# One level of Strassen's algorithm for the gate and up products of 20 of 22 column chunks per FFN, and an order planned with other matmul prices

## The chip, the cores and the metric

The kernel runs on one core of a Trainium2 chip. The metric is the device time of one execution in microseconds (us); before the change its median is 1421.67 us. TensorE multiplies matrices, VectorE, ScalarE and GpSimd work on tiles elementwise, and SyncE (SP in the profile) issues the DMA transfers between the chip's memory (DRAM) and SBUF. TensorE reads its operands from SBUF and writes its sums into PSUM, of which this kernel uses 8 banks of 128 x 512 numbers.

## The reference

A trunk of two layers on 512 tokens of width 1024, in float32. Each layer has a mixer (attention of one kind or another), a cross attention to 256 memory tokens, and an FFN; each adds its normed output to x. Only the FFN and the norm ahead of it are touched:

```python
def swiglu(h, wg, wu, wd):
    return (jax.nn.silu(h @ wg) * (h @ wu)) @ wd

for layer in range(DEPTH):
    ...
    y = swiglu(rms_norm(x, g[4]), ffn_wg[layer], ffn_wu[layer], ffn_wd[layer])
    x = x + rms_norm(y, g[5])
```

wg and wu are 1024 x 2816, wd is 2816 x 1024. The width 2816 is cut into 22 chunks of 128 columns.

## The kernel before

**Two numbers for one.** TensorE takes fp32r operands. To keep float32's precision, every operand is split into a high part (ScalarE's copy into fp32r) and a low part (VectorE's subtraction); `split` (line 556) issues the two. `mm` (line 509) then makes three matmuls of one: high by high, high by low, low by high, each with a weight load of its own. All partitions are 128, and the sum over 1024 has 8 steps (`KO`).

**The FFN** (`ffn`, line 999). `hT` holds the normed activations, transposed: 8 steps x 512 tokens, high and low. `up(c)` makes chunk c: it loads 128 columns of wg and of wu (`w_group`: one raw buffer of 512 KB each, of three; split into high and low, two w buffers each, of eight), and multiplies each with hT into a PSUM bank of its own, 8 steps x 3 matmuls with 512 moving columns. Chunks 0 and 1 go in two halves of 256 tokens, as the first half of hT is ready earlier. Then come tanh on ScalarE, two VectorE steps that read PSUM, and a split whose subtraction is GpSimd's. Three chunks make a group (four in the last). After the next group's first chunk come the group's down products: for each block of 128 tokens and each half of the 1024 output columns a bank, into which the group's chunks are summed, 3 matmuls each of 512 columns, and which VectorE adds to `yacc` (ScalarE copies it in the first group).

**The way to the FFN.** Four blocks of 128 tokens go through `chain` (line 849): out projection, cross attention, norm. Its last stage, `norm_T` (line 632), scales a block, transposes it into two banks (`turn`) and splits each into hT.

**Buffers.** Tiles are taken by tag: raw 3 x 1024 numbers a partition, w 8 x 1024, u 20 x 1024 (activations of chunks, yacc, gains, some down weights), q 10 x 512, pt 4 x 1024 (down weights), and 8 PSUM banks.

**The order.** Nothing is issued while the program is written. `Plan.note` (line 135) records each instruction with what it depends on and a price in ns from `price` (line 182). `order` then simulates the engines, the buffers and the DMA queue in rounds: a backward pass gives each instruction a latest time, a forward pass starts on each engine what is ready, by that time; the best round's order is issued. `lend` (line 398) gives a VectorE addition, subtraction or product on SBUF to GpSimd, when GpSimd has nothing to do and the wait on VectorE is long. The order of each engine is fixed with that; on the chip only semaphores decide when an instruction starts. All instructions are issued by line 491, so the profile's rows tell them apart by tiles: `w` weights, `raw` loaded weights, `ps` PSUM, `q` and `u` the tags above.

Of the kernel before, what the change touches and what calls it, by code (L numbers as in the profile page):

```python
# [11 lines left out]
F32 = mybir.dt.float32  # L12
# [7 lines left out]
P = 128  # L20
# [67 lines left out]
class Plan:  # L88
# [46 lines left out]
    def note(self, eng, method, args, kw):  # L135
        aps = [("out" if i == 0 else "in", v) for i, v in enumerate(args) if isinstance(v, bass.AP)]
        if "out" in kw or "out_" in kw:
            aps = [("in", v) for _, v in aps]
        aps += [("out" if k in ("out", "accum_out") else "in", v) for k, v in kw.items() if isinstance(v, bass.AP)]

        op = dict(eng=eng.name, call=(eng, method, args, kw), cost=0.0, deps=set(), tiles=set(), prio=len(self.ops))
        i = len(self.ops)
        for kind, ap in aps:
            if ap.space == bass.MemoryType.DRAM and not str(ap.tensor.name).startswith("xsave"):
                continue
            name, p0, p1, mask = self.region(ap)
# [35 lines left out]
    def price(self, eng, method, args, kw, aps):  # L182
        n = max([self.free(a) for a in aps] + [1])
        if method == "dma_start":
            size = 1
            for _, k in aps[0].ap:
                size *= k
            return size * 4 / 360.0
        if eng == "tensor":
            if method == "transpose":  # L190
                return 107.0
            c = self.free(args[2]) / 2.4
            return max(25.0, 2.5 + (c if args[2].dtype == F32R else 4 * c))
        if eng == "scalar":
            extra = sum(isinstance(kw.get(k), bass.AP) for k in ("bias", "scale", "accum_out"))
            return (52 if aps[1].space == PSUM else 95) + 0.83 * n + 93 * extra
        if eng == "vector":
            psum = any(a.space == bass.MemoryType.PSUM for a in aps)
            n = n + 62 * sum(isinstance(v, bass.AP) and self.free(v) == 1 for v in args[2:3])
            if method == "reciprocal":  # L200
                return 60 + 8 * n
            if method in ("tensor_copy", "tensor_scalar", "memset") and not psum:
                return 65 + 0.52 * n
            return 65 + 1.04 * n
# [289 lines left out]
class Trunk:  # L494
# [11 lines left out]
    def tile(self, shape, dtype, tag, bufs=1):  # L506
        return self.nc.tile(self.sb, shape, dtype, tag, bufs)

    def mm(self, ps, L, R, first, last):
        (lh, ll), (rh, rl) = L, R  # L510
        mmul = self.nc.tensor.matmul
        mmul(ps, lh, rh, start=first, stop=False)
        mmul(ps, lh, rl, start=False, stop=False)
        mmul(ps, ll, rh, start=False, stop=last)

    def unit(self, dtype=F32R):
        return self.tile([P, 1024], dtype, "u", 20)
# [114 lines left out]
    def norm_T(self, src, g, dst, tb):  # L632

        r = self.rstd(src)
        hs = [self.qtile() for _ in range(2)]
        for i in range(2):
            self.nc.vector.scalar_tensor_tensor(hs[i], src[i], r, g[:, i * 512:(i + 1) * 512], op0=ALU.mult, op1=ALU.mult)
        self.turn(hs, dst, tb)

    def hT_tiles(self):  # L640
        return [self.tile([P, KO, T], F32R, f"hT{k}") for k in ("hi", "lo")]
# [207 lines left out]
    def chain(self, tb, c):  # L849
# [84 lines left out]
        yield  # L934
        if c["hT"] is None:
            c["hT"] = self.hT_tiles()
        self.norm_T(self.xhalves(x, tb), c["g"][2], c["hT"], tb)
        yield

    def first_heads(self, w, c):  # L940
# [24 lines left out]
    def last_heads(self, l, w, units, n, c, x_src, fill):  # L965


        a = self.a
        lead = LEAD if n > 2 else 1
        step = 8.0 / n  # L970

        def before():
            yield from fill
            yield from self.first_heads(w, c)
            c["g"] = [self.gain(a["sandwich_g"][l, 1:2, :])]
            c["wq"] = self.w_group(a["ca_wq"][l], 0, MEM, self.gcols(l))

        def block(tb):
            if tb == 0:
                c["x"] = []  # L980
            x = self.xtile()
            self.nc.sync.dma_start(x, x_src[tb * P:(tb + 1) * P, :])
            c["x"].append(x)
            yield from self.chain(tb, c)

        def rest():
            c["wo"] = [self.w_cols(a["ca_wo"][l], 0, 1, 1024, k) for k in range(2)]
            c["g"] += [self.gain(a["sandwich_g"][l, i:i + 1, :]) for i in (3, 4)]
# [7 lines left out]
        return c["x"], c["hT"]  # L996


    def ffn(self, l, x, hT):
        nc, a = self.nc, self.a  # L1000
        groups = [list(range(c, min(c + 3, NCH))) for c in range(0, NCH - 1, 3)]
        groups[-1].append(NCH - 1)
        acts = {}

        def up(c):
# [4 lines left out]
            for s in parts:  # L1010
                for ps, wf in ((pg, wg), (pu, wu)):
                    for ko in range(KO):
                        self.mm(ps[:, s], wf(ko), (hT[0][:, ko, s], hT[1][:, ko, s]), ko == 0, ko == KO - 1)
            th, b = self.qtile(), self.qtile()
            nc.scalar.activation(th, pg, AF.Tanh, scale=0.5)
            nc.vector.scalar_tensor_tensor(th, th, 1.0, pg, op0=ALU.add, op1=ALU.mult)
# [2 lines left out]
            nc.scalar.activation(at[:, 0:512], b, AF.Copy)  # L1019
            nc.gpsimd.tensor_sub(at[:, 512:1024], b, at[:, 0:512].bitcast(F32))  # L1020

        where = self.pt_tiles
        yacc = None
        up(0)
        for gi, grp in enumerate(groups):
            last = gi == len(groups) - 1
            for c in grp[1:]:
                up(c)
# [4 lines left out]
            if last:  # L1033
                g = self.gain(a["sandwich_g"][l, 5:6, :])
            else:
                up(groups[gi + 1][0])
# [557 lines left out]
    def run(self):  # L1594
# [4 lines left out]
        x, hT = self.mixer0(x)  # L1599
        blocks = self.ffn(0, x, hT)  # L1600
        x, hT = self.mixer1(x, blocks)
        for tb in self.ffn(1, x, hT):
# [43 lines left out]
```

## Time and profile before

| | |
|---|---|
| median of 3 runs | 1421.67 us (1420.76 to 1422.24) |
| the profiled execution | 1422.67 us |
| its span, first to last instruction | 1421.0 us |
| granted TensorE clock, mean | 0.996 |
| TensorE matmul busy | 1383.2 us (97%) |
| VectorE, ScalarE, GpSimd busy | 833.7, 725.0, 355.9 us |
| DMA moved | 132.05 MB, mean 93 GB/s |

The profile is one execution. Its times are us from the first instruction. PE is TensorE, PEld its weight loads, DVE VectorE, ACT ScalarE, POOL GpSimd. A matmul's row lasts longer than the time to the next matmul's start, since matmuls are pipelined: 0.39 us against 0.23 us for 512 columns. So throughput is read from starts and not from durations. A group `x2` of the timeline gives the start of the first and the time to the end of the last.

### The profile page before, as it was taken

Reading aid. Unit: us, or ns where it says so; the run is one execution under the profiler, and the core shown is the slowest. Engines: PE = TensorE matmul, PEld = TensorE weight load, DVE = VectorE, ACT = ScalarE, POOL = GpSimd, SP = SyncE. Lnnn points to the kernel's source line nnn. Section 1 sums busy time; section 2 is a strip of 40 time slices with the busy share of each in tenths; the row PEclk is TensorE's granted clock in tenths of the full one; section 3 lists DMA queues with packets and bytes.
Section 4 is the critical chain, followed back from the end, with each engine's and each line's share of the span. In section 5 each row is a group of like instructions: output and inputs, shape, how many; then the busy total and the mean of one; then the engine's idle time right before and its main releaser. Section 6 shows DMA issues by size and latency. Waiting matters only on the chain.

```text
span 1421.0 us, 21566 instructions
## 1 busy us (share of the span) xinstructions
PE 1383.2 (97%) x8003; PEld 1204.0 (85%) x8003; DVE 833.7 (59%) x1851; ACT 725.0 (51%) x1606; POOL 355.9 (25%) x429
## 2 busy tenths in 40 slices
PE   7999999999899999999999999999989999999997
PEld 6788988889788888888889999988878888888886
DVE  5667899498842333433466888876984233343344
ACT  5768879488643122223245677786863322222322
POOL 2203334244320121012031233312552012101202
PEclk9999999999999999999999999999999999999999
DMA  7251112321233233324321321243234323332411
GB/s 218 65 150 47 46 45 87 107 74 61 89 119 89 89 104 90 114 78 134 105 74 54 95 91 61 77 147 104 85 92 121 89 84 110 89 108 85 119 60 60
DMA packets 150425, 132.05 MB, mean 93 GB/s; under 512 B 6928, under 2 KB 134096, under 8 KB 150320
## 3 DMA queue, kind: packets, MB, share of 16 engines
q1 hardware_dynamic: 150320, 130.67, 30.2%
q8 instruction: 63, 1.03, 0.3%
q14 instruction: 42, 0.34, 0.1%
HBM read 126.26 MB, written 4.19 MB: 92 GB/s over the span
## 4 chain that ended last, share of the span: by engine, by line
PE 84%; DVE 7%; ACT 3%; DMA 2%; POOL 2%; issue 2%; SPq 0%; POOLq 0%; DVEq 0%; ACTq 0%
PE ps L491 84%; DVE q L491 2%; DVE x L491 1%; DVE u L491 1%; ACT q L491 1%; DVE c L491 1%; DMA raw<-in_ev_w_in_dram 1%; POOL c L491 1%; POOL q L491 1%; ACT u L491 1%; DVE pt L491 1%; DMA pt<-in_ev_w_in_dram 0%; DVE w L491 0%; ACT pt L491 0%; POOL x L491 0%
## 5 line engine op out<-in xcount | busy, mean ns | idle before, releaser
L491 PE MATMUL ps<-hThi,w 128*128 128x512 f32 (+1 forms) x1664 | 488.0, 375 | 2.6 <-DVE q L491 2.6
L491 PEld LDWEIGHTS ps<-hThi,w 128*128 128x128 f32 x1664 | 306.5, 190 | 58.3 <-ACT junk L491 1.6
L491 PE MATMUL ps<-hTlo,w 128*128 128x512 f32 (+1 forms) x832 | 311.6, 375 | 0.4 <-DVE hTlo L491 0.2
L491 PE MATMUL ps<-w,hThi 128*128 128x256 f32 (+2 forms) x1280 | 281.9, 316 | 2.3 <-ACT hThi L491 2.3
L491 DVE TENSOR_TENSOR w<-raw,w 128x1024 fp32r<-128x1024 f32 (+1 forms) x136 | 170.2, 1268 | 152.3 <-issue 72.8
L491 ACT ACTIVATE w<-raw 128x1024 fp32r<-128x1024 f32 (+1 forms) x153 | 158.4, 1051 | 164.4 <-PE ps L491 138.7
L491 PE MATMUL ps<-pt,u 128*128 128x512 f32 (+3 forms) x1126 | 231.8, 338 | 1.4 <-DVE pt L491 0.8
L491 PEld LDWEIGHTS ps<-w,hThi 128*128 128x128 f32 x1280 | 210.5, 192 | 15.2 <-ACT hThi L491 3.2
L491 DVE TENSOR_TENSOR u<-ps,u 128x512 f32<-128x512 f32 (+6 forms) x278 | 150.6, 546 | 116.4 <-PE ps L491 98.0
L491 PEld LDWEIGHTS ps<-pt,u 128*128 128x128 f32 (+1 forms) x1126 | 175.2, 173 | 31.6 <-DVE pt L491 1.5
L491 POOL TENSOR_TENSOR u<-q,u 128x512 fp32r<-128x512 f32 x44 | 64.0, 1454 | 542.7 <-ACT u L491 542.7
L491 PE MATMUL ps<-w,hTlo 128*128 128x256 f32 (+2 forms) x640 | 199.8, 313 | 0.0
L491 PE MATMUL ps<-u 128*128 128x512 f32 (+4 forms) x806 | 186.4, 348 | 0.1
L491 PEld LDWEIGHTS ps<-hTlo,w 128*128 128x128 f32 x832 | 158.0, 190 | 28.3 <-DVE hTlo L491 1.3
L491 PEld LDWEIGHTS ps<-u 128*128 128x128 f32 (+1 forms) x806 | 131.1, 183 | 18.4 <-DVE pt L491 0.4
L491 DVE SCALAR_TENSOR_TENSOR q<-q,ps 128x512 f32<-128x512 f32 x88 | 60.3, 686 | 141.1 <-PE ps L491 103.5
L491 ACT ACTIVATE u<-ps 64x256 fp32r<-64x256 f32 (+6 forms) x269 | 116.0, 438 | 51.8 <-PE ps L491 47.4
L491 ACT ACTIVATE q<-ps 128x256 f32<-128x256 f32 (+6 forms) x158 | 72.7, 460 | 119.0 <-PE ps L491 117.4
L491 PEld LDWEIGHTS ps<-w,hTlo 128*128 128x128 f32 x640 | 122.4, 192 | 7.2 <-DVE hTlo L491 0.8
L491 PE MATMUL ps<-ident,q 128*128 128x128 f32 (+1 forms) x645 | 109.6, 278 | 18.0 <-DVE q L491 13.8
L491 PEld LDWEIGHTS ps<-ident,q 128*128 128x128 f32 (+1 forms) x645 | 77.5, 141 | 28.3 <-DVE q L491 11.5
L491 ACT ACTIVATE q<-q,c 128x128 f32<-128x128 f32 (+3 forms) x160 | 88.7, 557 | 12.7 <-DVE c L491 11.8
(151 smaller groups left out, 1518.1 us busy)
## 6 DMA issues: line engine op xcount, KB each, us to landing
raw<-in_ffn_wg_dram SPq DMA_DIRECT2D x44, 512.0 KB
raw<-in_ffn_wu_dram SPq DMA_DIRECT2D x44, 512.0 KB
raw<-in_ffn_wd_dram SPq DMA_DIRECT2D x44, 512.0 KB
raw<-in_od_w_in_dram SPq DMA_DIRECT2D x24, 512.0 KB
raw<-in_ev_w_in_dram SPq DMA_DIRECT2D x16, 512.0 KB
u<-in_sandwich_g_dram SPq DMA_DIRECT2D x10, 512.0 KB
x<-in_x_dram SPq DMA_DIRECT2D x8, 512.0 KB
raw<-in_ev_w_out_dram SPq DMA_DIRECT2D x8, 512.0 KB
```

What stands on the lines that cost most here:

```text
L491: getattr(getattr(self.nc, self.eng[i]), method)(*args, **kw)
```

## The change

Chunks 0 and 1 stay. For each other chunk (`fast`), the four half products of gate and up are taken as one 2 x 2 block product: the activations in blocks of 512 sums x 256 tokens (A11, A12 for the first 256 tokens, A21, A22 for the others), the weights in blocks b11, b21 (wg) and b12, b22 (wu). Winograd's form of Strassen's algorithm makes it of 7 products of 4 steps, 3 matmuls each, with 256 moving columns: A11 b11, A12 b21, S1 t1, S2 t2, S3 t3, S4 b22, A22 t4.

- The weight sums t1 to t4 are made per chunk from the raw weights, two on GpSimd and two on VectorE, and every right factor is split on its own.
- The activation sums S1 = A21 + A22, S2 = S1 - A11, S3 = A11 - A21, S4 = A12 - S2 are made once per FFN in `norm_S`, which takes the place of norm_T there: blocks 0 and 1 are kept in float32, blocks 2 and 3 make the sums. S1, S2 and S4 take six u buffers. S3 is split by `third` ahead of chunk 2 into the place of A21 in hT, which only chunks 0 and 1 read.
- Two banks take the seven products, X and Z in one and Y in the other. Between them PSUM is read with p1 = X and with additions; gate g and up u then lie in SBUF, where the activation reads them.
- The prices: a matmul 13 ns beyond its columns (6.5 up to 100 ns of columns) in place of 2.5, a weight load 53 ns in place of 107 for 128 fp32r columns, a transpose 109 in place of 107, and 115 ns more for ScalarE and VectorE on 64 partitions.

```diff
+PLAIN = 2
+HALF_ROWS = 115
...
-        op["load"] = 53.0 if method != "matmul" else self.free(args[1]) / (1.2 if args[1].dtype == F32R else 2.4)
+        op["load"] = 53.0 if method != "matmul" else self.free(args[1]) / 2.4
...
-                return 107.0
+                return 109.0
             c = self.free(args[2]) / 2.4
-            return max(25.0, 2.5 + (c if args[2].dtype == F32R else 4 * c))
+            return max(25.0, (13.0 if c > 100 else 6.5) + (c if args[2].dtype == F32R else 4 * c))
+        half = HALF_ROWS if eng in ("scalar", "vector") and n > 100 and aps[0].ap[0][1] == DH else 0
...
+    def norm_S(self, src, g, c, tb):
...
+        if tb < 2:
+            c["keep"].append(self.unit(F32))
+        keep = [c["keep"][tb % 2][:, i * 512:(i + 1) * 512] for i in range(2)]
...
+            self.split(c["hT"][0][sl], c["hT"][1][sl], pt.rearrange("p (a b) -> p a b", b=P))
+            if tb < 2:
+                nc.scalar.activation(keep[i], pt, AF.Copy)
+            pts.append(pt)
+        if tb < 2:
+            return
...
+        nc.scalar.activation(a21, pts[0], AF.Copy)
+        nc.vector.tensor_add(s1, pts[1], a21)
+        nc.vector.tensor_sub(s2, s1, keep[0])
+        nc.vector.tensor_sub(keep[0], keep[0], a21)
+        nc.vector.tensor_sub(keep[1], keep[1], s2)
+        cs = slice((tb - 2) * P, (tb - 1) * P)
+        for n, t in ((1, s1), (2, s2), (4, keep[1])):
+            hi, lo = c["S"][n]
+            self.split(hi[:, :, cs], lo[:, :, cs], t.rearrange("p (a b) -> p a b", b=P))
...
+        def third():
+            for i in range(2):
+                cs = slice(i * P, (i + 1) * P)
+                hi, lo = blocks["S3"]
+                self.split(hi[:, :, cs], lo[:, :, cs], ops["keep"][i][:, 0:512].rearrange("p (a b) -> p a b", b=P))
...
+        def fast(c):
...
+            (b11, b21), (b12, b22) = [(r[:, 0:512], r[:, 512:1024]) for r in raw]
+            t1, t2, t3, t4 = [self.qtile() for _ in range(4)]
+            nc.gpsimd.tensor_sub(t1, b12, b11)
+            nc.vector.tensor_sub(t2, b22, t1)
+            nc.gpsimd.tensor_sub(t3, b22, b12)
+            nc.vector.tensor_sub(t4, b21, t2)
+            one, two = self.bank(), self.bank()
+            X, Z, Y = one[:, 0:256], one[:, 256:512], two[:, 0:256]
+
+            def product(ps, left, right, first):
+                wt = self.tile([P, 1024], F32R, "w", 8)
+                hi, lo = wt[:, 0:512], wt[:, 512:1024]
+                self.split(hi, lo, right)
+                ah, al = blocks[left]
+                for k in range(4):
+                    s = slice(k * P, (k + 1) * P)
+                    self.mm(ps, (hi[:, s], lo[:, s]), (ah[:, k, :], al[:, k, :]), first and k == 0, k == 3,
+                            skip_group_check=not first)
+
+            sums, u3, g, u = [self.qtile() for _ in range(4)]
+            p1, u2, u3 = sums[:, 0:256], sums[:, 256:512], u3[:, 0:256]
+            product(X, "A11", b11, True)
+            nc.scalar.activation(p1, X, AF.Copy)
+            product(Y, "S2", t2, True)
+            nc.vector.tensor_add(u2, Y, p1)
+            product(X, "A12", b21, False)
+            nc.scalar.activation(g[:, 0:256], X, AF.Copy)
+            product(Y, "S3", t3, False)
+            nc.vector.tensor_add(u3, Y, p1)
+            product(Z, "S1", t1, True)
+            nc.vector.tensor_add(u[:, 256:512], Z, u3)
+            product(Y, "A22", t4, False)
+            nc.vector.tensor_add(g[:, 256:512], Y, p1)
+            product(Z, "S4", b22, False)
+            nc.vector.tensor_add(u[:, 0:256], Z, u2)
+            finish(c, g, u)
+
+        def make(c):
+            if c == PLAIN:
+                third()
+            (up if c < PLAIN else fast)(c)
```

## Rows read from the trace of the kernel before

**Rows 1.** The page's first part: the span, and each engine's busy time.

```profile
span 1421.0 us, 21566 instructions
PE 1383.2 (97%) x8003; PEld 1204.0 (85%) x8003; DVE 833.7 (59%) x1851; ACT 725.0 (51%) x1606; POOL 355.9 (25%) x429
```

**Rows 2.** The chain that ended last: shares, two longest pieces (start, us, what).

```profile
PE 84%; DVE 7%; ACT 3%; DMA 2%; POOL 2%; issue 2%; SPq 0%; POOLq 0%; DVEq 0%; ACTq 0%
...
389.38 362.90 PE ps L491 x1696
...
1064.98 345.90 PE ps L491 x1568
```

**Rows 3.** Busy time by stretch: length, busy us (instructions) of each engine, clock, DMA.

```profile
360.00:389.00 29.00, 23.68 (x165) 21.61 (x163) 23.41 (x34) 16.87 (x37) 11.36 (x10) 0.88 0.36 109
...
1040.00:1065.00 25.00, 19.90 (x148) 17.83 (x145) 21.30 (x30) 15.46 (x32) 12.57 (x11) 1.00 0.38 116
...
600.00:700.00 100.00, 100.00 (x443) 82.84 (x442) 35.84 (x43) 24.05 (x29) 16.06 (x9) 1.00 0.35 103
```

**Rows 4.** Timeline of TensorE, first chunks of FFN 0 (start, us, engine, what).

```profile
395.10 0.40 PE L491 MATMUL ps<-hThi,w 128*128 128x256 f32 x2
...
397.26 0.40 PE L491 MATMUL ps<-hThi,w 128*128 128x256 f32 x2
...
400.97 0.62 PE L491 MATMUL ps<-hThi,w 128*128 128x512 f32 x2
...
404.38 0.62 PE L491 MATMUL ps<-hThi,w 128*128 128x512 f32 x2
```

**Rows 5.** Timeline of VectorE: instructions that follow one another.

```profile
311.18 0.67 DVE L491 TENSOR_TENSOR x<-ps,x 128x512 f32<-128x512 f32 x1
311.78 0.68 DVE L491 TENSOR_TENSOR x<-x,u 128x512 f32<-128x512 f32 x1
...
449.46 2.36 DVE L491 TENSOR_TENSOR w<-raw,w 128x1024 fp32r<-128x1024 f32 x2 [2.95 <-PE ps L491]
...
461.23 1.22 DVE L491 TENSOR_TENSOR w<-raw,w 128x1024 fp32r<-128x1024 f32 x1
...
```

**Rows 6.** One group by form (busy us, mean ns, idle before); one row of GpSimd's timeline.

```profile
L491 DVE TENSOR_TENSOR q<-ps,q 128x256 f32<-128x256 f32 x16 | 6.7, 422 | 2.4 <-ACT q L491 2.3
...
427.95 1.30 POOL L491 TENSOR_TENSOR u<-q,u 128x512 fp32r<-128x512 f32 x1 [7.59 <-ACT u L491]
```

**Rows 7.** Timeline of FFN 0: the end of a down product and its reader.

```profile
472.61 0.84 PE L491 MATMUL ps<-u 128*128 128x512 f32 x3
...
473.29 1.52 PE L491 MATMUL ps<-pt,u 128*128 128x512 f32 x6
473.49 0.69 DVE L491 TENSOR_TENSOR u<-ps,u 128x512 f32<-128x512 f32 x1 [1.29 <-PE ps L491]
```

**Rows 8.** Timeline of VectorE and GpSimd, FFN 0, where both work on SBUF.

```profile
397.82 3.46 DVE L491 TENSOR_TENSOR w<-raw,w 128x1024 fp32r<-128x1024 f32 x2
...
398.49 1.71 POOL L491 TENSOR_TENSOR u<-q,u 128x512 fp32r<-128x512 f32 x1 [18.00 <-ACT u L491]
...
465.84 1.23 DVE L491 TENSOR_TENSOR w<-raw,w 128x1024 fp32r<-128x1024 f32 x1 [3.39 <-issue]
...
466.06 3.27 POOL L491 TENSOR_TENSOR w<-raw,w 128x1024 fp32r<-128x1024 f32 x1 [2.46 <-PE ps L491]
```

**Rows 9.** Timeline of FFN 0: a weight load's issue and its first reader.

```profile
420.38 0.34 SPq L491 DMA_DIRECT2D raw<-in_ffn_wd_dram  x1
...
423.92 1.06 ACT L491 ACTIVATE u<-raw 128x1024 fp32r<-128x1024 f32 x1 [6.26 <-DMA raw<-in_ffn_wd_dram]
```

**Rows 10.** Timeline of ScalarE and VectorE: the last block's split into hT.

```profile
387.40 2.06 ACT L491 ACTIVATE hThi<-ps 128x512 fp32r<-128x512 f32 x4 [5.10 <-PE ps L491]
...
388.03 1.89 DVE L491 TENSOR_TENSOR hTlo<-ps,hThi 128x512 fp32r<-128x512 f32 x3 [3.82 <-ACT hThi L491]
```

More of the change, by code (lines that the diff above doesn't have):

```diff
@@ L190, in price @@
             if method == "transpose":
-                return 107.0
+                return 109.0
             c = self.free(args[2]) / 2.4
-            return max(25.0, 2.5 + (c if args[2].dtype == F32R else 4 * c))
+            return max(25.0, (13.0 if c > 100 else 6.5) + (c if args[2].dtype == F32R else 4 * c))
+        half = HALF_ROWS if eng in ("scalar", "vector") and n > 100 and aps[0].ap[0][1] == DH else 0
         if eng == "scalar":
             extra = sum(isinstance(kw.get(k), bass.AP) for k in ("bias", "scale", "accum_out"))
-            return (52 if aps[1].space == PSUM else 95) + 0.83 * n + 93 * extra
+            return (52 if aps[1].space == PSUM else 95) + 0.83 * n + 93 * extra + half
         if eng == "vector":
@@ L203, in price @@
                 return 65 + 0.52 * n
-            return 65 + 1.04 * n
+            return 65 + 1.04 * n + half
         if eng == "gpsimd":
@@ L507, in tile, with mm @@
         return self.nc.tile(self.sb, shape, dtype, tag, bufs)
-    def mm(self, ps, L, R, first, last):
+    def mm(self, ps, L, R, first, last, **kw):
         (lh, ll), (rh, rl) = L, R
         mmul = self.nc.tensor.matmul
-        mmul(ps, lh, rh, start=first, stop=False)
-        mmul(ps, lh, rl, start=False, stop=False)
-        mmul(ps, ll, rh, start=False, stop=last)
+        mmul(ps, lh, rh, start=first, stop=False, **kw)
+        mmul(ps, lh, rl, start=False, stop=False, **kw)
+        mmul(ps, ll, rh, start=False, stop=last, **kw)
     def unit(self, dtype=F32R):
@@ L638, in norm_T @@
         self.turn(hs, dst, tb)
+    def norm_S(self, src, g, c, tb):
+        nc = self.nc
+        r = self.rstd(src)
+        hs = [self.qtile() for _ in range(2)]
+        for i in range(2):
+            nc.vector.scalar_tensor_tensor(hs[i], src[i], r, g[:, i * 512:(i + 1) * 512], op0=ALU.mult, op1=ALU.mult)
+        if tb < 2:
+            c["keep"].append(self.unit(F32))
+        keep = [c["keep"][tb % 2][:, i * 512:(i + 1) * 512] for i in range(2)]
+        pts = []
+        for i in range(2):
+            pt = self.bank()
+            for j in range(4):
+                nc.tensor.transpose(pt[:, j * P:(j + 1) * P], hs[i][:, j * P:(j + 1) * P], self.ident)
+            sl = (slice(None), slice(i * 4, i * 4 + 4), slice(tb * P, (tb + 1) * P))
+            self.split(c["hT"][0][sl], c["hT"][1][sl], pt.rearrange("p (a b) -> p a b", b=P))
[4 more added lines that the diff above has]
+            return
+        if tb == 2:
+            c["S"] = {n: [self.unit().rearrange("p (k t) -> p k t", k=4) for _ in range(2)] for n in (1, 2, 4)}
+        a21, s1, s2 = [self.qtile() for _ in range(3)]
+        nc.scalar.activation(a21, pts[0], AF.Copy)
[7 more added lines that the diff above has]
+            self.split(hi[:, :, cs], lo[:, :, cs], t.rearrange("p (a b) -> p a b", b=P))
     def hT_tiles(self):
@@ L936, in chain @@
             c["hT"] = self.hT_tiles()
-        self.norm_T(self.xhalves(x, tb), c["g"][2], c["hT"], tb)
+            c["keep"] = []
+        self.norm_S(self.xhalves(x, tb), c["g"][2], c, tb)
         yield
@@ L995, in last_heads, with ffn @@
               *[(block(tb), [max(ready[tb], LATE + tb) + STAGE * s if s < 5 else max(ready[tb] + STAGE * s, LATE + tb + STAGE * s, ready[3] + 0.2 if s > 4 else 0) for s in range(9)]) for tb in range(NT)])
-        return c["x"], c["hT"]
-    def ffn(self, l, x, hT):
+        return c["x"], c
+    def ffn(self, l, x, ops):
         nc, a = self.nc, self.a
+        hT, S = ops["hT"], ops["S"]
+        blocks = {"A11": [t[:, 0:4, 0:256] for t in hT], "A12": [t[:, 4:8, 0:256] for t in hT],
+                  "A22": [t[:, 4:8, 256:512] for t in hT], "S3": [t[:, 0:4, 256:512] for t in hT],
+                  "S1": S[1], "S2": S[2], "S4": S[4]}
         groups = [list(range(c, min(c + 3, NCH))) for c in range(0, NCH - 1, 3)]
@@ L1013, in up, with finish @@
                         self.mm(ps[:, s], wf(ko), (hT[0][:, ko, s], hT[1][:, ko, s]), ko == 0, ko == KO - 1)
+            finish(c, pg, pu)
+        def finish(c, pg, pu):
             th, b = self.qtile(), self.qtile()
@@ L1020, in up @@
             nc.gpsimd.tensor_sub(at[:, 512:1024], b, at[:, 0:512].bitcast(F32))
+        def third():
+            for i in range(2):
+                cs = slice(i * P, (i + 1) * P)
+                hi, lo = blocks["S3"]
+                self.split(hi[:, :, cs], lo[:, :, cs], ops["keep"][i][:, 0:512].rearrange("p (a b) -> p a b", b=P))
+        def fast(c):
+            rows = lambda w: w[l].rearrange("(ko p) c -> p ko c", p=P)[:, :, c * P:(c + 1) * P]
+            raw = []
+            for w in ("ffn_wg", "ffn_wu"):
+                raw.append(self.tile([P, 1024], F32, "raw", 3))
+                self.loads.append(nc.sync.dma_start(raw[-1].rearrange("p (k c) -> p k c", c=P), rows(a[w])))
+            (b11, b21), (b12, b22) = [(r[:, 0:512], r[:, 512:1024]) for r in raw]
[32 more added lines that the diff above has]
+            finish(c, g, u)
@@ L1022, in ffn @@
+        def make(c):
+            if c == PLAIN:
+                third()
+            (up if c < PLAIN else fast)(c)
         where = self.pt_tiles
         yacc = None
-        up(0)
+        make(0)
         for gi, grp in enumerate(groups):
@@ L1027, in ffn @@
             for c in grp[1:]:
-                up(c)
+                make(c)
             wds = []
@@ L1035, in ffn @@
             else:
-                up(groups[gi + 1][0])
+                make(groups[gi + 1][0])
             if yacc is None:
@@ L1598, in run @@
         self.xsave = tc.nc.dram_tensor("xsave", (T, D), F32, kind="Internal").ap()
[L1599 to L1602, printed above, removed]
+        x, ops = self.mixer0(x)
+        blocks = self.ffn(0, x, ops)
+        x, ops = self.mixer1(x, blocks)
+        for tb in self.ffn(1, x, ops):
             for c in (slice(0, 512), slice(512, 1024)):
```

## The prediction

> **What bounds the kernel now.** I read the page from the top: TensorE is busy 97% of the span, the other engines 59% and less [rows 1]. A busy TensorE need not be the limit, so the chain of work that ended last comes next: 84% of it is TensorE, and its two longest pieces by far are the two FFNs, 362.9 us and 345.9 us in which nothing but matmuls stands on the chain [rows 2]. The busy time by stretch says the same: inside an FFN TensorE is busy 100 of 100 us, VectorE 36, ScalarE 24, GpSimd 16 [rows 3]. So half of the kernel is bound by the number of matmul columns and by nothing else, and what the change takes from TensorE there is gain, as long as the other engines keep up. The mixers are another matter: at their ends (360 to 389 us, 1040 to 1065 us) TensorE has gaps and VectorE is busy for 81% and 85% [rows 3]; there VectorE's work stands on the chain.
>
> **Part 1, the products.** A chunk now takes 2 x 8 x 3 = 48 matmuls of 512 columns. By the timeline, 15 of them start within 404.38 - 400.97 = 3.41 us, 0.227 us each; so 10.91 us a chunk [rows 4]. The new form takes 7 products x 4 x 3 = 84 matmuls of 256 columns. The kernel has such matmuls, in the same form and with a weight load each, in the first two chunks: 18 start within 397.26 - 395.10 = 2.16 us, 0.120 us each [rows 4]; 84 take 10.08 us. That is 0.83 us a chunk, and 40 chunks make -33 us. It is 7.6% and not 12.5%, since each matmul pays about 13 ns beyond its columns, and there are more matmuls. The Trainium skill ("TensorE: Matmul & The Clock Gate", Back-to-back issue gap) gives N/2.4 + 2.5 ns for N columns as the gap of isolated matmuls, by which 256 columns would take 109 ns and 512 columns 216 ns, and the gain would be 1.19 us a chunk or 47 us; the rows show 120 and 227 ns here, the measurement decides, and the sum does not use the rule.
>
> Down products (24 matmuls a chunk, 5.45 us) and the two plain chunks stay as they are. So a chunk with its share of down products goes from 16.4 to 15.5 us of TensorE.
>
> **Part 2, what the other engines get.** Count for one chunk. VectorE had 2 weight splits of 1024, two steps of the activation, one split of the down weights and 8/3 additions to yacc. Instructions that follow one another overlap a little: two of 1024 take 2.36 us, so 1.14 apart (1.22 alone), and two of 512 start 0.60 apart (0.68 alone) [rows 5]. That is 3 x 1.14 + 2 x 0.60 + 2.67 x 0.60 = 6.2 us in 16.4 us (the 36% of rows 3 are a little less, since GpSimd takes some splits). It gets 7 splits of 512, t2 and t4, five additions of 256 out of PSUM (0.42 us alone, about 0.34 in a row [rows 6]), and the activation: 11 x 0.60 + 5 x 0.34 = 8.3 us, with the unchanged part (1.14 + 1.6) 11.0 us of 15.5, or 71%. GpSimd goes from one subtraction of 512 to three, 1.3 us each undisturbed [rows 6], 3.9 us. ScalarE gets 7 copies of 512 for 2 of 1024 and two of 256; it stays near 40%. None of the three reaches TensorE's 15.5 us, so by throughput the matmuls cover all of it, at a price of nothing. If that cover is gone, each us of VectorE beyond 15.5 costs 40 us.
>
> **Part 3, the waits that are new.** The seven products alternate between two banks (X and Z lie in one, Y in the other), and each of the last five accumulates on, or writes beside, what is read from its bank. So TensorE may not go on in a bank before ScalarE (twice) or VectorE (three times) has read it. Meanwhile it has the other bank's product, 12 x 0.120 = 1.44 us. The way to the reader takes about 0.20 us (the last down matmul of a bank ends its turn at 473.29, VectorE starts at 473.49 [rows 7]), the read 0.42 [rows 6]; if the way back takes 0.20 too, an estimate, 0.62 us is left. A VectorE instruction of 512 in front of the read (0.60) just fits in. Queued behind a waiting TensorE stand the next product and the down products; behind a VectorE that waits for TensorE stand the splits of the next weights.
>
> What can break this: a VectorE instruction that reads two SBUF operands and a GpSimd one that reads SBUF do not run together. With GpSimd at work on a subtraction (398.49, 1.71 us), two VectorE splits took 3.46 us in place of 2.36; and with VectorE first, GpSimd's split took 3.27 us [rows 5, 8]. The order was not planned with this. Such work was 3.4 + 1.3 = 4.7 us of 16.4 (29%); now it is 11 x 0.60 + 1.14 = 7.7 on VectorE (the activation's operands have moved from PSUM to SBUF, too) and 3.9 on GpSimd, 75% of 15.5. I estimate: 120 GpSimd subtractions, half of which meet a VectorE instruction, cost some 1 us each; VectorE's free 4.5 us a chunk take most of that. Where a read that TensorE waits for stands behind (taken as every second time), up to 0.5 us past the 0.62 us reach TensorE, half of that on the mean. 60 x 0.5 x 0.25 = 7 us. Bounds: 0 (down products, which need none of this, fill the gaps) and 33 us (0.83 us a chunk, all of the gain). I take 7, nearer to 0, as FFN rows show TensorE without a gap beside collisions that exist already [rows 3, 8].
>
> Weights: both raw buffers of a chunk are now held until t2 to t4 are made and the last half is split, and there are three buffers. A reload takes 3.5 us to its first reader (420.38 to 423.92 [rows 9]), then t1 (1.3), t2 (0.6) and a split (1.1) come ahead of the second product: 6.5 us. Eight w buffers hold one chunk and one product, so the last split of a chunk can run before its first product starts, 10.1 us before the next chunk's. I cost it at nothing, with 3.6 us to spare; the DMA bytes stay the same, and SP's queue has the same issues, each waiting longer for its buffer.
>
> **Part 4, the sums of the activations.** norm_S adds two ScalarE copies for blocks 0 and 1, and for blocks 2 and 3 a copy, four VectorE additions and three splits; the S3 split comes before chunk 2. Per block 7 x 0.60 = 4.2 us on VectorE. Block 3's fall under the plain chunks' matmuls (over 11 us after the last hT split, at 388 [rows 10]), and VectorE is idle there by two thirds. Block 2's compete with block 3's norm on an engine busy for 81% [rows 3]: 0 if the planner puts them behind, 4.2 us a layer if they go first. One row speaks for little: ScalarE waited 5.1 us for block 3's transposes, with TensorE on other products [rows 10]. I take 1.5 a layer, +3, bounds 0 and 8.
>
> **Part 5, new prices.** They change the order everywhere, the mixers too, and no row shows how. The mixers' gaps outside the start and end are a few per cent, so a better or worse order is worth some us; I take 0, bounds -6 and +6.
>
> **Sum.** -33 + 7 + 3 + 0 = -23 us. The profiled execution took 1422.7 us (span 1421.0), the median is 1421.7; the difference is 1 us, and I go from the median: 1398.
>
> **Rivals.** (a) The exclusion of Part 3 turns into waits of TensorE: 0.4 to 0.8 us a chunk, 1408 to 1420. For it: 75% shared use, and that the planner lends VectorE's subtractions to GpSimd when VectorE has a queue, where they take twice as long (1.3 for 0.6). Against it: TensorE had not one gap at 29%, and VectorE has 4.5 us a chunk free. The Trainium skill ("SBUF — State Buffer", SBUF: two separate sides) calls it an exclusive lock held for the whole instruction; rows 8 agree, as the second VectorE split took just the rest of GpSimd's time longer. (b) Slower: weights come late. Place: the raw buffers and the second product of each chunk. It decides once the last split of a chunk runs later than 6.5 us before the next chunk's first product, that is if VectorE lags by more than 3.6 us; each us beyond costs up to 40 us, so at 1.5 us a chunk: 1398 + 60 less what the wait spares elsewhere (its 7 us of other stalls), some 1430 to 1450. For it: three buffers for a chunk's two and a down weight. Against it: down products are at hand as a filler, and the loads are issued 10 us ahead. (c) Hardly any stall and a better order in the mixers: below 1384.
>
> **How the numbers follow.** Forecast (1384 to 1408): 0.65. (a) 0.18, of which about a third ends within 0.2% (2.8 us, about what a measurement of this kernel can tell from no change). (b) 0.10. (c) 0.07. Faster: 0.65 + 0.07 + 0.12 = 0.84; same 0.06; slower 0.10. The range takes the forecast and most of (a): 1384 to 1419.
>
> **What would show it.** Right: in the FFN stretches matmuls of 256 columns 0.12 us apart, TensorE still near 100%, both FFNs shorter by 13 to 17 us each on the chain, VectorE at 65 to 80%. (a) would show TensorE idle in gaps of 0.2 to 1 us in the FFNs, ended by VectorE's q or u, beside VectorE subtractions of 1.5 us and more in place of 0.68. (b) would show ScalarE and VectorE waiting for raw, and gaps of over 1 us at each chunk's second product. Part 4 is wrong if the stretch from the last head to the first dense matmul grows by more than 3 us. Wrong altogether if 256-column matmuls with moving operands from the S tiles do not keep 0.12 us.

## The result, and the profile after

The change makes the kernel slower: 1486.86 us median (1485.46 to 1489.55, 4 runs) against 1421.95 us (1420.76 to 1424.85, 4 runs); ratio 1.0456, 95% interval 1.0434 to 1.0477. The prediction said 1398 us, with 1384 to 1419 as the range and 0.10 for slower. The size and the sign are wrong.

The page of the changed kernel, first part and chain, beside [rows 1] and [rows 2]:

```profile
span 1483.7 us, 25658 instructions
PE 1386.0 (93%) x9443; PEld 1261.4 (85%) x9443; DVE 1149.2 (77%) x2336; ACT 850.3 (57%) x1914; POOL 490.6 (33%) x536
...
PE 63%; DVE 18%; issue 6%; DMA 6%; ACT 4%; POOL 4%; SPq 0%; POOLq 0%; DVEq 0%; ACTq 0%
```

TensorE was 84% of the chain and is 63%; VectorE has gone from 7% to 18%. The FFNs' two pieces of over 340 us are gone: the longest piece of matmuls that is left in an FFN is 34.5 us. By stretch, as in [rows 3]:

```profile
400.00:425.00 25.00, 18.29 (x115) 16.92 (x115) 25.00 (x26) 12.38 (x24) 15.25 (x10) 0.80 0.19 54
...
450.00:650.00 200.00, 184.61 (x1258) 168.76 (x1256) 155.95 (x221) 84.44 (x145) 58.36 (x40) 0.99 0.33 93
...
1150.00:1350.00 200.00, 186.33 (x1256) 169.91 (x1255) 153.38 (x213) 84.77 (x146) 61.13 (x42) 0.99 0.32 93
```

In the FFNs TensorE is busy for 185 of 200 us. The busy time still flatters it, since a matmul's row is longer than its turn; the count of matmuls does not. VectorE, at 78%, is far from full. At the head of the first FFN it is worse: TensorE is busy for 18 of 25 us, VectorE spends all 25 us on 26 instructions (in run e11 below, 23.6 us on 42), and the granted clock is 0.80 on the mean, a mixture of 2.4 and 1.2 GHz.

Where the 63 us of span lie, by stages. An FFN is taken from its first matmul to the last addition of 512 columns to yacc (start times in the timeline), so what lies between two FFNs is mixer:

| us | before | after | difference |
|---|---|---|---|
| mixer 0 | 370.7 | 377.0 | +6.3 |
| FFN 0 | 381.1 | 399.1 | +18.0 |
| mixer 1 | 297.0 | 306.3 | +9.3 |
| FFN 1 | 362.0 | 391.3 | +29.3 |
| tail | 10.1 | 10.0 | -0.1 |

Both FFNs should have been 16.6 us shorter (half of the 33 us of products). They are 18 and 29 us longer, so they have lost 35 and 46 us.

Not all of that is idle time. In places the granted clock fell as well, as here at the head of the first FFN:

```profile
405.00:410.00 5.00, 2.17 (x15) 1.76 (x14) 5.00 (x5) 1.67 (x3) 2.33 (x2) 0.94 0.00 0
410.00:415.00 5.00, 2.70 (x12) 2.41 (x12) 5.00 (x7) 3.46 (x7) 2.84 (x2) 0.50 0.36 105
415.00:420.00 5.00, 5.00 (x26) 4.77 (x25) 5.00 (x7) 2.17 (x4) 3.11 (x3) 0.54 0.00 0
```

At 0.50, which is 1.2 GHz, a matmul of 256 columns starts every 0.21 us in place of 0.12 (kernel before, 373 to 378 us). Read in steps of 2 us, the changed kernel's FFNs have 27 us of matmul time at that clock, in seven places; e11, with the same matmuls, has none. By the two rates that is some 12 us, an estimate. The runs below with more idle time have more of it (39 us in e4, 6 us in e2).

What ends the gaps stands in the waits of the stretch from 450 to 650 us (engine, what it waited for, us in total, times, longest):

```profile
POOL q L494 <- DMA raw<-in_ffn_wu_dram: 72.3, 11, 20.0
...
PEld ps L494 <- DVE q L494: 19.8, 19, 2.6
...
PE ps L494 <- DVE q L494: 15.1, 18, 2.3
```

TensorE and its weight loads wait for VectorE's q, which is the result of an addition out of PSUM: the hand-off between two products of one bank. TensorE's idle time in the stretch is 15.4 us by its rows, and 15.1 of them are this wait; none is a wait for split weights. The timeline shows one such wait (GpSimd, VectorE and TensorE; start, us):

```profile
528.91 2.99 POOL L494 TENSOR_TENSOR q<-raw 128x512 f32<-128x512 f32 x2 [1.67 <-DMA raw<-in_ffn_wu_dram]
531.85 1.73 POOL L494 TENSOR_TENSOR w<-raw,w 128x512 fp32r<-128x512 f32 x1
...
529.57 1.17 DVE L494 SCALAR_TENSOR_TENSOR q<-q 128x512 f32<-128x512 f32 x1 [0.81 <-ACT q L494]
530.67 1.77 DVE L494 TENSOR_TENSOR q<-raw,q 128x512 f32<-128x512 f32 x1
532.37 0.41 DVE L494 TENSOR_TENSOR q<-ps,q 128x256 f32<-128x256 f32 x1
532.70 1.43 DVE L494 TENSOR_TENSOR q<-raw,q 128x512 f32<-128x512 f32 x1
...
529.58 2.20 PE L494 MATMUL ps<-u,w 128*128 128x256 f32 x17
532.83 2.30 PE L494 MATMUL ps<-u,w 128*128 128x256 f32 x17 [1.05 <-DVE q L494]
```

GpSimd makes t1 and t3 from 528.91 on, and then a split that the planner lent to it. Meanwhile a step of the activation takes 1.17 us and t2 takes 1.77, where 0.68 is the time undisturbed. Only then, at 532.37, can VectorE read PSUM, and TensorE, idle for 1.05 us, goes on at 532.83. GpSimd's three instructions follow one another, so one VectorE instruction after the other is held up: 0.5, 1.1 and 0.75 us within 5 us.

How long VectorE is held up in all, its groups by form tell (mean ns in the third place), 450 to 650 us:

```profile
L494 DVE TENSOR_TENSOR w<-q,w 128x512 fp32r<-128x512 f32 x48 | 37.2, 786 | 2.7 <-ACT w L494 2.4
L494 DVE TENSOR_TENSOR q<-raw,q 128x512 f32<-128x512 f32 x23 | 29.6, 1287 | 3.6 <-POOL q L494 3.6
L494 DVE TENSOR_TENSOR w<-raw,w 128x512 fp32r<-128x512 f32 x31 | 26.4, 857 | 1.4 <-ACT w L494 1.3
L494 DVE TENSOR_TENSOR q<-ps,q 128x256 f32<-128x256 f32 x59 | 24.3, 416 | 7.9 <-PE ps L494 7.7
L494 DVE SCALAR_TENSOR_TENSOR q<-q 128x512 f32<-128x512 f32 x23 | 17.6, 766 | 3.3 <-ACT q L494 3.2
```

All forms of 512 columns with two SBUF operands are above their 0.68 us; the reads of PSUM keep their 0.42 us. 48 x 0.10 + 23 x 0.60 + 31 x 0.17 + 23 x 0.08 = 26 us in 200 us.

### The profile page after: what moved, and what is told of

It is laid out like the page before. It is cut to its first block, busy times and chain, and to the rows that moved or that the text cites. A ratio compares the mean times of both kernels' runs of the same rounds, so it can differ in the third digit from the quotient of the medians.

```text
span 1483.7 us, 25658 instructions
## 1 busy us (share of the span) xinstructions
PE 1386.0 (93%) x9443; PEld 1261.4 (85%) x9443; DVE 1149.2 (77%) x2336; ACT 850.3 (57%) x1914; POOL 490.6 (33%) x536
## 4 chain that ended last, share of the span: by engine, by line
PE 63%; DVE 18%; issue 6%; DMA 6%; ACT 4%; POOL 4%; SPq 0%; POOLq 0%; DVEq 0%; ACTq 0%
PE ps L494 63%; DVE q L494 8%; DVE w L494 5%; DMA raw<-in_ffn_wu_dram 4%; POOL q L494 2%; DVE u L494 2%; DVE x L494 1%; ACT w L494 1%; ACT q L494 1%; DVE pt L494 1%; ACT junk L494 1%; POOL c L494 1%; DMA x<-in_x_dram 1%; DMA raw<-in_ffn_wg_dram 1%; ACT u L494 1%
## 5 line engine op out<-in xcount | busy, mean ns | idle before, releaser
L494 PE MATMUL ps<-hThi,w 128*128 128x256 f32 (+1 forms) x1664 | 348.1, 297 | 27.3 <-DVE q L494 21.5
L494 PE MATMUL ps<-hTlo,w 128*128 128x256 f32 (+1 forms) x832 | 244.2, 295 | 1.6 <-DVE hTlo L494 1.6
L494 PE MATMUL ps<-u,w 128*128 128x256 f32 x1440 | 200.9, 287 | 32.7 <-DVE q L494 28.6
L494 PEld LDWEIGHTS ps<-w,hThi 128*128 128x128 f32 x1280 | 212.0, 194 | 14.6 <-ACT hThi L494 2.9
L494 PEld LDWEIGHTS ps<-u,w 128*128 128x128 f32 x1440 | 185.3, 194 | 41.7 <-DVE q L494 36.1
L494 POOL TENSOR_TENSOR q<-raw 128x512 f32<-128x512 f32 x80 | 117.3, 1487 | 297.7 <-DMA raw<-in_ffn_wu_dram 249.6
L494 ACT ACTIVATE w<-raw 128x512 fp32r<-128x512 f32 (+2 forms) x193 | 149.5, 787 | 97.1 <-PE ps L494 68.4
L494 DVE TENSOR_TENSOR w<-raw,w 128x512 fp32r<-128x512 f32 (+2 forms) x177 | 185.0, 1053 | 22.6 <-ACT w L494 16.4
L494 ACT ACTIVATE w<-q 128x512 fp32r<-128x512 f32 x160 | 99.5, 627 | 115.2 <-PE ps L494 76.2
L494 ACT ACTIVATE u<-ps 64x256 fp32r<-64x256 f32 (+5 forms) x277 | 120.3, 442 | 58.3 <-PE ps L494 54.4
L494 DVE TENSOR_TENSOR w<-q,w 128x512 fp32r<-128x512 f32 x156 | 123.4, 804 | 10.7 <-ACT w L494 9.9
```

The lines of the kernel that those rows point to most:

```text
L494: getattr(getattr(self.nc, self.eng[i]), method)(*args, **kw)
```

## The experiments

Theory L: VectorE's instructions with two SBUF operands and GpSimd's that read SBUF shut each other out; the reads of PSUM stand behind the instruction that was held up; TensorE, which may not go on in a bank that isn't read, waits. Its rivals: the weights come late (R), VectorE has too much to do (D), or it is the chain from load over t1 to t2 that holds VectorE up, and not the sharing (C).

One table holds the same view of every run, the stretch from 450 to 650 us in the first FFN. "Held up" is worked out as above, from VectorE's groups of 512 columns and their 0.683 us in e2. The matmuls of the stretch stand for TensorE's rate; their mix of widths differs a little between runs. "FFNs" is the length of both FFNs, as in the table of stages: every edit has the whole kernel planned anew, and the mixers move by several us with it, so what an edit does to the cause is read there (before: 743.2; e11: 709.1).

| run | GpSimd busy, us | VectorE busy | held up | matmuls | FFNs, us | median, us |
|---|---|---|---|---|---|---|
| after | 58.4 | 156.0 | 26 | 1258 | 790.4 | 1486.9 |
| e1 sums on VectorE, no lending | 18.0 | 167.6 | 4 | 1382 | 737.3 | 1424.1 |
| e2 nothing on GpSimd | 0 | 171.3 | 0 | 1399 | 721.1 | 1405.9 |
| e3 a bank for each product | 77.0 | 174.6 | 29 | 1360 | 735.1 | 1423.6 |
| e4 no reload | 79.1 | 154.6 | 35 | 1243 | 806.0 | 1497.4 |
| e5 = e2 and GpSimd reads | 49.4 | 180.5 | 21 | 1310 | 761.9 | 1446.0 |
| e6 = e2 and GpSimd writes | 40.8 | 169.2 | 0 | 1392 | 723.9 | 1412.2 |
| e7 = e2 and e3 | 0 | 180.7 | 0 | 1412 | 716.6 | 1401.6 |
| e8 no lending | 53.7 | 158.4 | 21 | 1278 | 779.7 | 1465.6 |

e1 to e6 and e8 are one run each, beside the kernel before at 1421.6 and 1421.3 us. The ten runs of one kernel (e10) spread over 6 us, so e6's 6 us above e2 may be nothing; the other differences that the argument uses are 10 us and more. L had the direction right each time, but its ranges held only in e5, e6 (at the edge), e7 and e12; e1, e2, e3 and e8 came out faster than their ranges, e11 too, and e4 slower.

**e1, the sums on VectorE.** The diff; the flag `keep` is also set around the split of the down weights:

```diff
-            nc.gpsimd.tensor_sub(t1, b12, b11)
+            nc.vector.tensor_sub(t1, b12, b11)
...
-            nc.gpsimd.tensor_sub(t3, b22, b12)
+            nc.vector.tensor_sub(t3, b22, b12)
...
-        if eng.name == "vector" and method in ("tensor_sub", "tensor_add", "tensor_mul") and op["cost"] > self.FLEX \
+        if not getattr(self, "keep", False) and eng.name == "vector" and method in ("tensor_sub", "tensor_add", "tensor_mul") and op["cost"] > self.FLEX \
...
+            nc.keep = True
             (up if c < PLAIN else fast)(c)
+            nc.keep = False
```

> The sums t1 and t3 go from GpSimd to VectorE, and in the FFNs no VectorE instruction is lent to GpSimd; GpSimd keeps one subtraction a chunk. VectorE's own work grows from 11.0 to 12.2 us of 15.5 a chunk. Theory L (VectorE and GpSimd shut each other out on SBUF, VectorE's reads of PSUM stand behind the instruction that was held up, TensorE waits for them; in the first FFN of the changed kernel VectorE lost 43 us that way and TensorE 42): two thirds of the held-up time goes, each FFN gets 20 to 30 us shorter, 1487 to some 1430 to 1445. Theory R (weights come late, since raw is held longer): no change beyond 5 us, as the raw buffers are held as long. Theory D (VectorE simply has too much to do, with the two-bank hand-off): slower, 1490 to 1520.

1424.1 us, 63 us less (53 of them in the FFNs), though VectorE has more to do. D falls; L's range was 1430 to 1445, so it is more than L had said. R is not out by this run: its forecast was no change, but t1 takes 0.68 us on VectorE where GpSimd took 1.46, so the raw buffers come free earlier, too. e4 decides on R.

**e2, GpSimd without work in the fast chunks.** e1 and:

```diff
-            nc.gpsimd.tensor_sub(at[:, 512:1024], b, at[:, 0:512].bitcast(F32))
+            nc.vector.tensor_sub(at[:, 512:1024], b, at[:, 0:512].bitcast(F32))
```

> As e1, and the low part of the activation goes to VectorE too: GpSimd has nothing to do in the fast chunks; VectorE 12.8 us of 15.5 a chunk. Theory L: VectorE's long instructions disappear altogether; both FFNs together 10 to 20 us shorter than in e1, 1415 to 1430. Theory R: as the changed kernel, 1480 to 1490. Theory D: slower than e1.

1405.9 us, 15.7 us below the kernel before and below L's range; the FFNs are 69 us shorter than in the changed kernel. Two views of it, the busy times of the stretch and VectorE's groups by form in it:

```profile
450.00:650.00 200.00, 199.40 (x1399) 187.42 (x1398) 171.28 (x295) 88.72 (x157) 0.00 (x0) 1.00 0.34 102
```

```profile
L494 DVE TENSOR_TENSOR w<-q,w 128x512 fp32r<-128x512 f32 x52 | 34.0, 683 | 1.0 <-ACT w L494 1.0
...
L494 DVE TENSOR_TENSOR q<-raw,q 128x512 f32<-128x512 f32 x26 | 17.7, 682 | 0.0
```

t2 and t4 take 0.682 us where they took 1.287. With VectorE busy for 86% and GpSimd for nothing, TensorE has hardly a gap: one engine with all of the work is better here than two that share it.

**e3, a bank for each product.** GpSimd keeps its sums; the sum that two products had in common goes to VectorE:

```diff
+            def alone(left, right):
+                ps = self.bank()[:, 0:256]
+                product(ps, left, right, True)
+                return ps
...
+            nc.scalar.activation(p1, alone("A11", b11), AF.Copy)
+            nc.vector.tensor_add(u2, alone("S2", t2), p1)
+            nc.vector.tensor_add(g[:, 0:256], alone("A12", b21), p1)
+            nc.vector.tensor_add(u3, alone("S3", t3), u2)
+            z = alone("S1", t1)
+            nc.vector.tensor_add(u[:, 256:512], z, u3)
+            nc.vector.tensor_add(u2, z, u2)
+            nc.vector.tensor_add(g[:, 256:512], alone("A22", t4), u3)
+            nc.vector.tensor_add(u[:, 0:256], alone("S4", b22), u2)
```

> Each of the seven products gets a bank of its own, and what two products shared is added by VectorE (two additions of 256 more, one ScalarE copy less); GpSimd keeps its sums. So no product waits until PSUM is read. Theory L: the held-up VectorE no longer stops TensorE at once, but only when no split weights are left; half of the FFNs' 80 us of gaps goes, 1440 to 1460. Theory R: no change, 1480 to 1490. Theory D: as L or better.

1423.6 us. VectorE is held up as long as in the changed kernel (t2 and t4 1.00 us, splits 0.84 and 0.90), but TensorE feels little of it. The stretch's busy times, and t2 and t4 among VectorE's groups:

```profile
450.00:650.00 200.00, 197.00 (x1360) 185.09 (x1360) 174.57 (x259) 83.94 (x142) 77.04 (x50) 0.98 0.36 107
```

```profile
L494 DVE TENSOR_TENSOR q<-raw,q 128x512 f32<-128x512 f32 x24 | 24.1, 1002 | 4.3 <-POOL q L494 4.3
```

So the loss needs both: instructions that are held up, and a hand-off that passes it on. In the FFNs, e2 without the first wins back 69 us and e3 without the second 55 us, of the 81 us by which the changed kernel's FFNs are longer than e11's. L had said half for e3; it is two thirds.

**e4, no reload.**

```diff
-        acts = {}
+        acts, kept = {}, []
...
-            for w in ("ffn_wg", "ffn_wu"):
+            if c > PLAIN:
+                raw = kept
+            for w in ("ffn_wg", "ffn_wu")[:2 * (c == PLAIN)]:
...
+            kept[:] = raw
```

> Leaves out the loads of the gate and up weights behind chunk 2: every fast chunk takes the raw weights that chunk 2 loaded, so no weights of a fast chunk can come late. All other instructions stay. Theory R: TensorE's gaps in the FFNs go, 1405 to 1430. Theory L: the gaps stay, since GpSimd's sums still meet VectorE's, 1470 to 1490.

1497.4 us: with no fast chunk's weights to wait for, it is slower by 10 us (16 in the FFNs), and TensorE's waits in the stretch are for VectorE's q (17.1 of 17.4 us). R falls. The planner lent more to GpSimd (busy for 79 us in place of 58), and VectorE's splits of raw weights take 1.10 us; by the table the held-up time rose from 26 to 35 us. So GpSimd's 72.3 us of waiting for the load, shown above, are not what holds TensorE up.

**e5 and e6, GpSimd work that nobody waits for.** Both are e2 and one addition:

```diff
+            spare = u3[:, 256:512]
...
+            for i in range(4):
+                nc.gpsimd.tensor_sub(spare, raw[i % 2][:, 0:256], raw[i % 2][:, 256:512])
```

```diff
             product(Z, "S4", b22, False)
+            for i in range(6):
+                nc.gpsimd.memset((t1, t3)[i % 2], 0.0)
```

> e2 with four subtractions of 256 on GpSimd added to every fast chunk, of raw weights, into a place that nobody reads; nobody waits for them. Theory L (the two shut each other out by their reads of SBUF): VectorE's instructions of 512 get up to 0.7 us longer again, TensorE's gaps come back, 1406 to some 1425 to 1450. Theory C (it is the chain, VectorE's t2 behind GpSimd's t1 behind the load, that costs): as e2, 1402 to 1410.

> e2 with six memsets of 512 on GpSimd added to every fast chunk, on weight sums whose splits are done; about the same GpSimd time as in e5, but without a read of SBUF. Theory L in the form that the reads collide: as e2, 1402 to 1412. If any GpSimd work on SBUF collides with VectorE's: as e5. The weight sums' tiles are held a little longer, which may cost up to 5 us.

1446.0 and 1412.2 us. The subtractions, whose result is read by nothing, take back 40 us of e2's gain, all of it in the FFNs (41 us); the memsets, with 40.8 us of GpSimd time in the stretch against 49.4, 6 us, of which 3 lie in the FFNs. The first two rows are e5's, the last two e6's:

```profile
L494 DVE TENSOR_TENSOR q<-raw,q 128x512 f32<-128x512 f32 x24 | 20.9, 871 | 0.0
...
L494 POOL TENSOR_TENSOR q<-raw 128x256 f32<-128x256 f32 x48 | 49.4, 1030 | 146.3 <-DMA raw<-in_ffn_wg_dram 66.1 <-DMA raw<-in_ffn_wu_dram 39.7 <-DVE u L494 17.8
```

```profile
L494 DVE TENSOR_TENSOR q<-raw,q 128x512 f32<-128x512 f32 x26 | 17.7, 682 | 0.0
...
L494 POOL MEMSET q<- 128x512 f32 x78 | 40.8, 527 | 164.1 <-DVE w L494 129.4 <-ACT w L494 31.7
```

C falls as the main cause: there is no chain in e5. (The added subtractions hold the raw buffers longer, too, but VectorE waits for loads for only 1.0 us of the stretch.) How much t2's wait for t1 adds in the changed kernel was not tried apart; VectorE waits there for GpSimd's q for 3.6 us in 200. In e5, 3.4 of TensorE's 7.3 us of idle time in the stretch end with q, at the hand-off, and 3.4 with u, the split activation, which comes behind VectorE's steps. And it is GpSimd's reads of SBUF that matter, since the memsets leave VectorE at 0.682 us. The Trainium skill ("SBUF — State Buffer", SBUF: two separate sides) says the same: a VectorE instruction with two SBUF inputs contends only with a GpSimd one that reads SBUF, and whichever starts first holds the ports for the whole instruction. The timeline above fits that: t2, begun at 530.67, lasts until 0.54 us behind the end of GpSimd's t3 at 531.90. The memsets' 6 us (at the edge of the expected range), if they are more than the spread, may come from t1's and t3's tiles, which are held longer; that wasn't tried apart.

**e8, no lending.** The changed kernel with e1's flag alone.

> The changed kernel with t1 and t3 on GpSimd as they were, but no VectorE instruction of the FFNs lent to GpSimd. Theory L: lent ones were 5 of 40 GpSimd instructions in 200 us, so a tenth of the 80 us of gaps goes, 1475 to 1485; the rest is t1 and t3. If lending were the main part: 1430 to 1450.

1465.6 us, 21 us less, where 2 to 12 were expected. But only 11 of them lie in the FFNs; the other 10 lie in the mixers, in which this edit leaves lending as it was. So lending is about an eighth of the FFNs' 81 us, close to the tenth that was expected: the lent instructions are few (5 of 40 on GpSimd). With t1 and t3 taken from GpSimd as well, e1 wins back 53.

**e7, both remedies,** e2 and e3 in one.

> e2 and e3 in one: a bank for each product, and GpSimd without work in the fast chunks; VectorE 13.5 us of 15.5 a chunk. Theory L with the hand-off: the two are the two halves of one cause, and e2 has only 4.2 and 1.2 us of gaps left in the stretches of its FFNs looked at; so 3 to 8 us below e2, 1398 to 1403. Theory D (VectorE has too much to do): no gain over e2, 1406 to 1415.

1401.6 us (4 runs; ratio to before 0.9854, interval 0.9834 to 0.9874). TensorE is busy for 200.00 of 200 us, VectorE for 180.7, and it is below D's 1406 to 1415: D's last ground is gone.

**e9 and e10, the mixers' part.** e9 is the kernel before with the new prices; e10 is the changed kernel with `PLAIN = 22`, so with prices and sums of activations and without a fast chunk.

> The kernel before with the new prices alone (half-filled partitions, matmuls, weight loads, transposes); no Strassen, no sums. From the changed kernel, to the last split into hT the first mixer took 3.5 us longer and the second 9.5 us; if the prices make that, 1428 to 1436; if the sums of activations make it, 1418 to 1425. The prediction took 0 (bounds -6 and +6) for the prices.

> The changed kernel with all 22 chunks plain: new prices, the sums S1 to S4 are made and S1, S2, S4 are never used; third never runs. Against e9 it shows what the sums cost at the two ends of the mixers: 0 to 8 us by the prediction, which took 3; so e9 + 3. If the sums make the 13 us of the mixers: e9 + 8 to + 15.

e9: 1430.5 us, ratio 1.0052 (1.0037 to 1.0068). e10: 1423.6 us, 1.0013 (1.0004 to 1.0023). The prices by themselves cost some 8 us, and the sums cost nothing that shows: e10, which has more to do, is 7 us faster than e9, where the prediction's +3 would have made it slower.

The 8 us lie in the mixers (378.3 and 299.4 us in the table's terms), and most of mixer 0's share is the clock. Between 174 and 210 us e9's TensorE has 13 us of matmul time at the lower clock (the granted clock is 0.50 from 175 to 180 us), worth some 6 us by the rates above; the kernel before has none in mixer 0, and e10, whose mixer 0 takes 373.2 us, has 3 us. The changed kernel's mixer 0 has 10 us of it (0.50 from 175 to 180 us, 0.59 from 180 to 185), worth some 5 of its +6 us. Its mixer 1 has none, so the +9 us there are something else, and stay open: e7's mixer 1, with the same prices and sums, takes 297.3 us where the changed kernel's takes 306.3. Which of the prices makes an order in which the clock falls stays open, too.

**e11 and e12, no lending anywhere.** e11 is e7, e12 the kernel before, each with

```diff
-    FLEX, MORE, HOLD = 100.0, 1.5, 5000.0
+    FLEX, MORE, HOLD = 1.0e9, 1.5, 5000.0
```

> e7 with lending off in the whole kernel, the mixers too: VectorE keeps some 60 additions and subtractions that GpSimd took. In the FFNs there is none left, so they stay. Theory L: in the mixers, where GpSimd has other work that VectorE meets, fewer collisions, 0 to 5 us less than e7, 1397 to 1402. If VectorE's load bounds the ends of the mixers more than the collisions do: 1402 to 1410.

> The kernel before with lending off in the whole kernel; nothing else is changed. In its FFNs TensorE has no gap with lending, so they stay. Theory L for the mixers: of the 9 us that e11 won on e7, most comes here too, 1412 to 1419. If e11's gain is one of another order only: 1419 to 1428.

e11: 1392.6 us, ratio 0.9794 (0.9778 to 0.981), 29 us below the kernel before and faster than both kernels. e12: 1413.4 us, 0.9929 (0.9913 to 0.9946): 10 us of it do without Strassen. e12's stages take 366.2, 377.8, 296.6 and 361.0 us: most of the gain lies in mixer 0 (4.6 us) and in FFN 0 (3.4 us), whose first matmuls run beside the end of the mixer. FFN 0's part is the clock: in the kernel before the granted clock is 0.50 from 373 to 378 us, with 6 us of matmul time at the lower level, worth some 3 us; in e12 it is 1.00 through the whole FFN. In mixer 0 TensorE stands still for 14.7 us in place of 19.0; how much of that is fewer collisions and how much another order, these runs do not separate.

e11's page, to hold against the first fence:

```profile
span 1390.0 us, 25701 instructions
PE 1356.1 (98%) x9443; PEld 1246.9 (90%) x9443; DVE 1164.5 (84%) x2621; ACT 839.1 (60%) x1874; POOL 230.8 (17%) x331
...
PE 85%; DVE 9%; DMA 2%; POOL 1%; ACT 1%; issue 1%; SPq 0%; POOLq 0%; DVEq 0%; ACTq 0%
```

With the same 9443 matmuls TensorE is 85% of the chain again. Its FFNs take 363.2 and 345.9 us, 17.9 and 16.1 us less than before, and 14.6 and 15.1 us less than e12's.

## Why the prediction was wrong, step by step

**What bounds the kernel: right for before, not for after.** "As long as the other engines keep up" was the condition, and it was checked by throughput alone.

**Part 1, -33 us: right.** Where nothing holds TensorE up, e11's FFNs are 34 us shorter than before, at 0.12 us a matmul. Some 3 us of that are the clock at the head of FFN 0; against e12, which has no lending and no lower clock in its FFNs either, it is 30 us.

**Part 2, loads: right and not to the point.** VectorE at 71% was forecast, and 78% by row time shows in the changed kernel, 13 points of which are time held up; it runs without harm at 90% in e7. The load was never the limit.

**Part 3, the stalls: the step that failed.** The mechanism was named, the price was 7 us, and it is some 80: against e11's the FFNs lost 35.9 + 45.4 us, of which some 70 are waiting and some 12 the lower clock, a term that the prediction did not have. Three parts of the waiting were mis-sized.
- The time held up: 60 meetings of 1 us were assumed. Worked out as above over both FFNs it is 108 us. The lent splits were left out of the sum, and e8 puts them at some 11 us of the FFNs.
- How much of it TensorE feels: an eighth was assumed, on the ground that only 0.62 us of slack must be passed, by one held-up instruction at a time. But t1, t3 and a lent split run one behind the other, so the delays add up within one hand-off, as the timeline shows. Some two thirds of the held-up time arrived at TensorE (about 70 of 108 us); e3, with a hand-off that doesn't pass it on, gives back 55 us of the FFNs with VectorE held up as before (110 us).
- "Down products fill the gaps": TensorE's order is fixed before the kernel runs, by prices that know nothing of the collisions. A filler that stands behind the waiting product in that order fills nothing. (This is argued from how the order is made; no run tries it.)

The bound of 33 us was wrong, too. It was set to "all of the gain", which is not a bound: nothing kept the waits below what the products save. A bound from the rows was at hand: 3 instructions of 1.3 us a chunk, each of which may hold VectorE up for its whole length, 40 x 3.9 = 156 us.

"FFN rows show TensorE without a gap beside collisions" was true and proved little: before, no product went on in a bank that had to be read first.

**The late weights (b):** given as the way to slower, and not the one; e4, without any of their loads, has the same gaps.

**Part 4, +3 us:** e10 against the kernel before shows 1.5 us for sums and prices together; not apart from the order's chance. VectorE was not idle by two thirds where block 3's sums were to fall (400 to 425 us: busy for 19.1 of 25 us in e10), but e10's FFNs are no longer for it (738.9 us against 743.2). **Part 5, 0 with bounds of 6:** e9 shows +8, outside, most of it the lower clock in mixer 0, which no term priced.

**The rival (a)** was the cause, with 0.4 to 0.8 us a chunk where 2 was right, and its end at 1420 was where the term's false bound had put it. Its signs were there: gaps ended by VectorE's q (0.8 us on the mean and up to 2.3, where 0.2 to 1 was forecast), beside subtractions of 1.29 us on the mean and up to 1.77.

## What to carry to other kernels

Before work is shared out between VectorE and GpSimd, add up the time of those instructions that exclude each other, both engines together, and ask what stands behind one that is held up; if a read that TensorE waits for does, GpSimd's subtraction at 1.3 us may cost more than VectorE's at 0.6 (e2: 15.7 us faster than before, the change as it was: 65 slower). Where products accumulate in turn in a few banks, give each its own bank if there are enough (e3: 63 us less than the changed kernel, with VectorE held up as long). And a static order hides nothing that its prices don't know: bound a new wait by the length of what can cause it, not by the gain it would eat. Look at the granted clock, stage by stage, before a difference of a few us is put down to the order of the work.

## What the runs showed of the hardware that was not expected

A GpSimd memset beside VectorE's subtractions costs VectorE nothing (0.682 us with 40.8 us of memsets in 200 us), a GpSimd subtraction of 256 columns takes 1.03 us there on the mean and lengthens VectorE's t2 and t4 to 0.87. Beside gaps of 1.5 and 1.35 us at the head of the changed kernel's FFN 0 (406 to 410 us) the granted clock fell to 0.50 and stayed there until about 419 us; in e11, without such gaps, it was 1.00 throughout. Not every gap does this: 2.3 us of idle time from 390 to 395 us, in the same kernel, left it at 1.00. Such stretches are worth several us, by the estimates above: some 12 us in the changed kernel's FFNs, some 5 us in the changed kernel's mixer 0 and some 3 us in the FFN 0 of the kernel before.
